# A two-layer hybrid block on one core: TensorE's build-time order made with a clock that counts each product's fixed part and each change of the array's form, and a new table of waits

## The chip, the cores and the metric

One core of one Trainium2 chip. The time is device microseconds of one execution of the whole program on that core. The kernel before has a median of 1361.12 us over three runs (1359.09 to 1361.54). Engines: TensorE (PE in the profile, its weight loads PEld), VectorE (DVE), ScalarE (ACT), GpSimd (POOL) and SyncE (SP), which issues most DMAs.

## The reference

Two layers of a block of a latent diffusion model. Its input are 256 latent rows and 256 context rows of 1024 numbers; the output are the latent rows after both layers.

```
for each layer:
  h  = adaLN(rms_norm(x));  hc = adaLN(rms_norm(ctx))      # scale, shift, gate from c and c_ctx
  A  = latent attention: q from a rank-256 part, k and v from a rank-128 part, 8 heads, rotary part
  B  = neighbourhood attention over a grid, window and context together, 8 heads, bias
  C  = Hyena: short convolution, two long convolutions (filters from a small MLP, by FFT)
  D  = gated linear attention, forward and backward, 4 heads, chunks of 64
  each branch * silu(its z) -> projection to 1024 -> * sigmoid(merge gate), summed
  x  = x + gate * rms_norm(sum @ w_out);   ctx likewise, in the first layer only
```

Context rows see only context rows in A and B; latent rows see both. All input and result types are fp32.

## The kernel before, in words

Nearly all of PE's time goes to products in fp32r. A factor `a` is split into a rounded part `ah` and a remainder `al` (for the incoming rows `hh` and `hl`, for weights `wh` and `wl`, for branch results `gh` and `gl`), and a product is three: `ah bh + ah bl + al bh`. The rounded part is a cast on ScalarE (L422, for weights L439 in `piece`), the remainder a subtraction on VectorE or GpSimd (`sub`, L380). Weights come as raw pieces of 512 KB through a pool of three buffers (`raw`, also `adaw` for adaLN); eight buffers hold split weights. PSUM has three pools: two buffers for the projections (`pj`, `pc`, `br`, `wo`), four for intermediate sums (`pa`, `sc`, `atp`, `go`, `ada`), two for transposes and small products (`ht`, `pt`, `ktp`, `kv`, `adat`).

PE's order is fixed while the program is built. Every part of the work is a generator that issues instructions and yields. A task that yields a number may go on when that many microseconds of PE's reckoned time have passed; `drive` (L312) takes the first task by priority that may go on, and where none may, it sets the reckoned clock to the earliest. The clock is moved by `mm` (L389: 512 columns of fp32r count 512/2400 = 0.2133 us; some callers pass a `cost`) and by `tr` (L403: 0.107 for a transpose). The numbers that tasks yield are in the table `WAIT` (L207), by name and layer; each stands for the time that other engines take before PE can use their result. The lowest priority has the long row of projections, branch products and merge gates of `layers`, which so fills the time of the others. Only PE's order is fixed like that (`manual_schedule`); the scheduler of the language sets the order of the other engines and queues for the PE order that it finds.

The tasks that matter here:

- `norm_in` (L633) turns the incoming rows, four groups of four transposes `ht` for each of the two streams. Behind each group VectorE and ScalarE apply scale and shift (`h`, L666 on ScalarE), ScalarE casts `hh`, and VectorE (second and fourth group) or GpSimd forms `hl`. Waits: `norm`, `norm_turn` ahead of the groups, `norm_step` between them.
- `latent_in` (L883) multiplies the turned rows by the weights of the low-rank parts (`pa`): it takes the four groups in turn. Behind it `latents` (L897) copies the parts `kr`, `xt` out of PSUM.
- `filters` makes the Hyena filters, products `f`, with waits `filt_...`.
- `ada_first` forms the first layer's scale and shift (`ada`, then two VectorE instructions `rows`, then `adat`), `ada_rest` (L600) the remaining parts, spaced by `ada_gap` and `ada_sum`.
- `unit` (L811) is one piece of attention: scores `sc`, maximum (L824), exponential (L826), scaling of `p` (L387), the wait `probs` or `probs2`, transposes `pt` and their copies. `q` in the first branch needs weights `wuq`, cast on ScalarE.
- `gla_dir` (L1238) is one direction of the linear attention for two heads: transposes `ktp`, a copy `kT` on ScalarE (L1270), the wait `gla_kT`, products `kv`, a chain of VectorE instructions `ut` over the chunks (L1289, L383), masked scores `atp`, four masking copies `at` on VectorE (L1314), the waits `gla_at` and `gla_scores`, and the products `go`, which need `at`.

Of the kernel before, what the change touches and what calls it, by code (L numbers as in the profile page):

```python
# [10 lines left out]
F32R = mybir.dt.float32r  # L11
# [114 lines left out]
def _layout(x, c, ctx, c_ctx, ada_w, ada_b, pre_g, post_g, w_in, mla_q_norm, mla_w_uq, mla_kv_norm, mla_w_ukv, na_rpb,  # L126
# [78 lines left out]


WAIT = {  # L207
    "ada_at0": (3.68, 7.47),
    "ada_at1": (6.0, 11.0),
    "ada_at2": (15.0, 17.0),  # L210
    "ada_at3": (17.5, 19.5),
    "ada_sum": (1.34, 0),
    "ada_load": (7.75, 9.57),
    "ada_gap": (4.19, 8.22),
    "norm": (3.44, 4.0),
    "norm_turn": (6.66, 5.25),
    "norm_ab": (0.16, 0.69),
    "norm_step": (0.65, 0.52),
    "filt_in": (3.1, 4.0),
    "filt_sin1": (6.0, 15.54),  # L220
    "filt_sin2": (6.0, 4.8),
    "filt_w3": (4.0, 4.49),
    "filt_step": (0.48, 0.82),
    "filt_sum": (10.0, 11.8),
    "filt_norm": (7.2, 15.6),
    "filt_dft": (0.3, 0.5),
    "filt_out": (1.82, 4.04),
    "probs": (5.63, 6.08),
    "probs2": (7.2, 7.7),
    "probs_out": (1.36, 0.94),  # L230
    "values_out": (1.14, 5.3),
    "latent_in": (2.81, 1.5),
    "latents": (10.0, 11.79),
    "latents_out": (5.62, 0.49),
    "mla_keys": (1.6, 1.78),
    "mla_v": (0.32, 0),
    "mla_k": (0.8, 2.25),
    "mla_q": (0.15, 0),
    "mla_q_out": (1.7, 1.04),
    "na_in": (2.87, 0.97),  # L240
    "hy_turn": (1.49, 4.79),
    "hy_turn_step": (0.35, 0.5),
    "hy_turn_out": (0.5, 0.67),
    "hy_dft": (1.57, 2.98),
    "hy_product": (12.59, 11.95),
    "hy_mid": (0.35, 0.81),
    "hy_out_step": (0.72, 0),
    "hy_order": (6.38, 0.9),
    "hy_out": (1.3, 1.0),
    "gla_in": (2.65, 0.67),  # L250
    "gla_logit": (1.02, 0.1),
    "gla_decay": (7.1, 2.9),
    "gla_dir": (6.31, 4.0),
    "gla_norm": (14.0, 4.73),
    "gla_turn": (0.03, 0.45),
    "gla_out": (1.66, 1.98),
    "gla_keys": (6.49, 5.03),
    "gla_kT": (0.9, 1.07),
    "gla_at": (0.5, 0.5),
    "gla_scores": (5.09, 7.57),  # L260
    "gla_o": (2.0, 1.05),
    "merged": (4.6, 3.55),
    "merged_step": (0.48, 0),
    "merged_out": (0.82, 1.24),
    "norm_first": (3.27, 8.0),
}


class Task:
    def __init__(self, gen, prio, ready):  # L270
        self.gen, self.prio, self.ready, self.cond, self.done = gen, prio, ready, None, False


class Block:
# [4 lines left out]
    def __init__(self, ctx, tc, dram, out):  # L279
        self.tc, self.nc, self.d, self.out = tc, tc.nc, dram, out  # L280
        pool = lambda name, bufs, **kw: ctx.enter_context(tc.tile_pool(name=name, bufs=bufs, **kw))
        self.const = pool("const", 1)
        self.small = pool("small", 1)
        self.hp = pool("hp", 1)
        self.mg = pool("mg", 4)
        self.raw = pool("raw", 3)
        self.wp = pool("wp", 8)
        self.gt = pool("gt", 8)
        self.gy = pool("gy", 4)
        self.s = pool("s", 20)  # L290
        self.tp = pool("tp", 15)
        self.tiny = pool("tiny", 6)
        self.dr = pool("dr", 1, space=bass.MemoryType.DRAM)
        self.pmm = pool("pmm", 2, space=bass.MemoryType.PSUM)
        self.pa = pool("pa", 4, space=bass.MemoryType.PSUM)
        self.pt = pool("pt", 2, space=bass.MemoryType.PSUM)
        self.n = 0
        self.clock = 0.0
        self.l = 0
        self.tasks = []  # L300
        self.ab = [self.small.tile([P, 2, 2, KT], F32, tag=f"ab{l}", name=f"ab{l}") for l in range(DEPTH)]
# [87 lines left out]
    def mm(self, out, lhsT, rhs, start=True, stop=True, skip=False, cost=None):  # L389
        self.nc.tensor.matmul(out, lhsT, rhs, start=start, stop=stop, skip_group_check=skip)  # L390
        if cost is None:
            cols = 1
            for w in rhs.shape[1:]:
                cols *= w
            cost = cols / 2400 if rhs.dtype == F32R else 4 * max(cols, 64) / 2400
        self.clock += cost

    def mm3(self, out, l, r, start, stop):
# [3 lines left out]

    def tr(self, out, in_):  # L403
        self.nc.tensor.transpose(out, in_, self.ident)  # L404
        self.clock += 0.107

    def rstd_of(self, halves):
# [1188 lines left out]
```

## Time and profile before

| | |
|---|---|
| median of 3 runs (lowest, highest) | 1361.12 us (1359.09, 1361.54) |
| the profiled execution, its span | 1358.52 us, 1356.7 us |
| granted TensorE clock, mean | 0.993 |
| PE busy | 1299.6 us, 96% |
| VectorE, ScalarE, GpSimd busy | 66%, 45%, 23% |
| DMA | 171.08 MB, 126 GB/s on the mean |

The times stand from the span's start. A row of a timeline gives the start, the duration, the engine, the line of the kernel, the operation, the result and its sources without their numbers, and in brackets how long the engine had stood idle before it and what ended that. Matmuls are pipelined: the distance of two starts is what one costs in a row of them. A line of a helper (L377, L380, L383, L387, L390, L404) serves many callers, so the names of the tiles tell the place.

### The profile page before, as it was taken

How to read it: one execution, taken by the hardware profiler on the slowest of the kernel's cores; microseconds unless marked ns; L12 is line 12 of the kernel's file. 1: busy time of each engine (PE TensorE's matmuls, PEld its weight loads, DVE VectorE, ACT ScalarE, POOL GpSimd, SP SyncE). 2: the span in 40 equal slices, each digit the busy share in tenths (PEclk: the TensorE clock that was granted, in tenths of full speed). 3: DMA queues.
4: the chain of work that ended last, by engine and by line, in shares of the span. 5: the costliest groups of instructions: out<-in, count | busy, mean ns of one | idle time of the engine just before them, and what ended most of it. 6: DMA issues, size and time to landing. Idle time of an engine off the chain costs nothing. (4 is left out here: it accounts for less than half of the span.)

```text
span 1356.7 us, 20161 instructions
## 1 busy us (share of the span) xinstructions
PE 1299.6 (96%) x7444; PEld 1023.7 (75%) x7444; DVE 889.4 (66%) x1660; ACT 607.1 (45%) x1282; POOL 318.3 (23%) x408
## 2 busy tenths in 40 slices
PE   5999999999999999999999999899999999999996
PEld 3877677777777776778767778787767899678875
DVE  5778666575143547676476597887579776768864
ACT  4655556233233332222344444575475456434552
POOL 2332213333030101124111123342123421121210
PEclk9999999999999999999999999999999999999999
DMA  9521222233243433324422352432135366434361
GB/s 350 214 93 40 93 70 77 94 110 109 94 155 124 145 120 108 124 94 139 142 77 80 114 192 85 138 106 99 48 115 158 115 211 212 156 101 153 118 208 63
DMA packets 55507, 171.08 MB, mean 126 GB/s; under 512 B 7470, under 2 KB 10128, under 8 KB 55408
## 3 DMA queue, kind: packets, MB, share of 16 engines
q1 hardware_dynamic: 49056, 153.31, 34.1%
q0 software_dynamic: 5440, 16.16, 3.8%
q8 instruction: 59, 0.97, 0.3%
q10 hardware_dynamic: 912, 0.31, 0.1%
q14 instruction: 40, 0.33, 0.1%
HBM read 163.45 MB, written 6.31 MB: 125 GB/s over the span
## 5 line engine op out<-in xcount | busy, mean ns | idle before, releaser
L380 DVE TENSOR_TENSOR wl<-raw,wh 128x512 fp32r<-128x512 f32 (+1 forms) x416 | 299.0, 740 | 191.2 <-ACT wh L439 186.3
L439 ACT CAST wh<-raw 128x512 fp32r<-128x512 f32 (+1 forms) x416 | 248.5, 617 | 285.1 <-DMA raw<-in_w_in 156.2
L390 PE MATMUL pc<-hh,wh 128*128 128x256 f32 (+1 forms) x688 | 239.8, 349 | 2.1 <-DVE kr L906 1.5
L390 PE MATMUL pc<-hh,wl 128*128 128x256 f32 (+1 forms) x688 | 229.8, 334 | 0.0
L390 PE MATMUL pc<-hl,wh 128*128 128x256 f32 (+1 forms) x688 | 229.3, 333 | 0.0
L390 PE MATMUL pj<-wh,hh 128*128 128x512 f32 x512 | 212.7, 415 | 1.5 <-ACT wh L439 0.8
L390 PE MATMUL pj<-wl,hh 128*128 128x512 f32 x512 | 200.6, 392 | 0.8 <-DVE wl L380 0.6
L390 PE MATMUL pj<-wh,hl 128*128 128x512 f32 x512 | 200.3, 391 | 0.0
L390 PEld LDWEIGHTS pc<-hh,wh 128*128 128x128 f32 x688 | 131.2, 191 | 25.6 <-issue 10.9
L390 PEld LDWEIGHTS pc<-hl,wh 128*128 128x128 f32 x688 | 131.2, 191 | 13.8 <-issue 2.4
L390 PEld LDWEIGHTS pc<-hh,wl 128*128 128x128 f32 x688 | 130.8, 190 | 13.3
L390 PEld LDWEIGHTS pj<-wh,hh 128*128 128x128 f32 x512 | 96.2, 188 | 32.3 <-issue 12.5
L390 PEld LDWEIGHTS pj<-wl,hh 128*128 128x128 f32 x512 | 96.4, 188 | 23.2 <-DVE wl L380 3.6
L390 PEld LDWEIGHTS pj<-wh,hl 128*128 128x128 f32 x512 | 96.1, 188 | 20.9
L380 POOL TENSOR_TENSOR gl<-y,gh 128x256 fp32r<-128x256 f32 (+1 forms) x44 | 36.6, 839 | 302.7 <-ACT gh L422 287.3
L826 ACT ACTIVATE p<-sc,mx 128x512 f32<-128x512 f32 (+1 forms) x96 | 59.0, 616 | 57.9 <-DVE mx L824 54.0
L390 PE MATMUL br<-wh,gh 128*128 128x512 f32 x192 | 77.2, 402 | 2.3 <-DVE gt L383 2.3
L390 PE MATMUL br<-wl,gh 128*128 128x512 f32 x192 | 75.1, 391 | 1.6 <-DVE wl L380 1.6
L390 PE MATMUL br<-wh,gl 128*128 128x512 f32 x192 | 74.9, 390 | 0.0
L1347 ACT ACTIVATE gt<-pj 128x512 f32<-128x512 f32 x48 | 28.6, 596 | 93.2 <-PE pj L390 93.0
L824 DVE TENSOR_REDUCE mx<-sc 128x1 f32<-128x512 f32 (+1 forms) x96 | 55.1, 591 | 11.5 <-PE sc L390 10.6
L377 POOL TENSOR_TENSOR merged<-merged,gt 128x512 f32<-128x512 f32 x24 | 33.1, 1385 | 83.8 <-DVE gt L383 83.8
(286 smaller groups left out, 2213.9 us busy)
## 6 DMA issues: line engine op xcount, KB each, us to landing
raw<-in_w_in SPq DMA_DIRECT2D x160, 512.0 KB, 3.6
adaw<-in_ada_w SPq DMA_DIRECT2D x36, 512.0 KB, 3.8
raw<-in_w_branch SPq DMA_DIRECT2D x32, 512.0 KB, 3.6
raw<-in_w_out SPq DMA_DIRECT2D x16, 512.0 KB, 4.4
adaw<-in_ada_w SPq DMA_DIRECT2D x24, 256.0 KB, 5.2
H<-filt POOLq DMA_DIRECT2D x16, 256.0 KB, 4.0
nab<-in_na_bias POOLq DMA_DIRECT2D x16, 256.0 KB, 3.0
raw<-in_w_in SPq DMA_DIRECT2D x8, 448.0 KB, 4.2
```

What stands on the lines that cost most here:

```text
L377: eng.tensor_tensor(out=out, in0=a, in1=b, op=ALU.add)
L380: eng.tensor_tensor(out=out, in0=a, in1=b, op=ALU.subtract)
L390: self.nc.tensor.matmul(out, lhsT, rhs, start=start, stop=stop, skip_group_check=skip)
L439: nc.scalar.copy(hi, raw[:, sl])
L824: nc.vector.tensor_reduce(out=mx, in_=ps[h][:, :nk], axis=AX.X, op=ALU.max, negate=True)
L826: nc.scalar.activation(p[h][:, :nk], ps[h][:, :nk], AF.Exp, bias=mx, scale=1.0, accum_out=sm)
L1347: self.nc.scalar.activation(gates[s, t], ps, AF.Tanh, scale=0.5)
```

## The change

No instruction is added or taken away, and all tiles, pools and engines are as before; a row's line numbers are 1 to 8 higher. What differs is the order in which `drive` issues PE's instructions, and with it the order that the scheduler gives the other engines.

The clock gets a fixed part of 32 columns for each fp32r product without a `cost` of its own, and 0.1 us wherever the form of the array differs from that of the product before: its rows (64 or 128) or its columns (32, 64 or 128).

```diff
         self.clock = 0.0
+        self.mode = (128, 128)
...
-            cost = cols / 2400 if rhs.dtype == F32R else 4 * max(cols, 64) / 2400
+            cost = (cols + 32) / 2400 if rhs.dtype == F32R else 4 * max(cols, 64) / 2400
+        mode = (64 if lhsT.shape[0] <= 64 else 128, 32 if out.shape[0] <= 32 else 64 if out.shape[0] <= 64 else 128)
+        if mode != self.mode:
+            self.mode = mode
+            cost += 0.1
         self.clock += cost
...
     def tr(self, out, in_):
         self.nc.tensor.transpose(out, in_, self.ident)
+        if self.mode != (128, 128):
+            self.mode = (128, 128)
+            self.clock += 0.1
         self.clock += 0.107
```

In the table most entries rise by about 6%. Those that move otherwise are, in the first layer, `ada_sum`, `ada_gap` (4.19 to 1.65), `norm`, `norm_turn`, `filt_sin2`, `mla_v`, `na_in`, `hy_mid`, `gla_turn` (0.03 to 1.89), `gla_kT`, `gla_at`, `gla_scores`, and in the second `ada_at1`, `norm`, `norm_step`, some of `filt_...`, `na_in`, `hy_mid`, `gla_keys`. Two of its lines:

```diff
-    "norm": (3.44, 4.0),
-    "gla_scores": (5.09, 7.57),
+    "norm": (4.8, 3.77),
+    "gla_scores": (4.1, 8.02),
```

Three places show what the new order does. The first is PE at the boundary of the layers, where the second layer begins: `ht` is the fourth group of transposes of the second stream, `pa` its products with the low-rank weights, `pc` a projection, `f` a product of the filters. Before:

```order
L390 MATMUL pa_8356<-wl_8089,hh_8202 128x192
L390 MATMUL pa_8356<-wh_8088,hl_8203 128x192
L404 MATMUL ht_8395<-ident,xn_8181 128x128
L404 MATMUL ht_8395<-ident,xn_8192 128x128
L404 MATMUL ht_8395<-ident,xn_8181 128x128
L404 MATMUL ht_8395<-ident,xn_8192 128x128
L390 MATMUL pa_8357<-wh_8088,hh_8202 128x192
L390 MATMUL pa_8357<-wl_8089,hh_8202 128x192
L390 MATMUL pa_8357<-wh_8088,hl_8203 128x192
L390 MATMUL pa_8357<-wh_8088,hh_8202 128x192
L390 MATMUL pa_8357<-wl_8089,hh_8202 128x192
L390 MATMUL pa_8357<-wh_8088,hl_8203 128x192
```

The same four transposes in the new order:

```order
L409 MATMUL ht_8366<-ident,xn_8169 128x128
L409 MATMUL ht_8366<-ident,xn_8180 128x128
L409 MATMUL ht_8366<-ident,xn_8169 128x128
L409 MATMUL ht_8366<-ident,xn_8180 128x128
L391 MATMUL f_2067_8378<-w3h_8134,a_1888_7688 128x512
L391 MATMUL f_2067_8378<-w3l_8135,a_1888_7688 128x512
L391 MATMUL pc_8359<-hh_7888,wh_8351 128x256
L391 MATMUL pc_8359<-hl_7889,wh_8351 128x256
L391 MATMUL pc_8359<-hh_7888,wl_8352 128x256
L391 MATMUL pc_8359<-hh_7888,wh_8351 128x256
L391 MATMUL pc_8359<-hl_7889,wh_8351 128x256
L391 MATMUL pc_8359<-hh_7888,wl_8352 128x256
```

Before, `pa` follows the fourth group at once, and six `pa` stand ahead of it; now two `f` and twelve `pc` (six of them shown) stand between the fourth group and the first `pa`.

The second place is ScalarE at the start of the program, around the casts `wh` of the first weights and the scaled rows `h`. Before:

```order
L666 ACTIVATE h_116_397<-ht_392,ab_99 128x256
L422 CAST hh_299<-h_114_387 128x2x256
L422 CAST hh_299<-h_116_397 128x2x256
L439 CAST wh_207<-raw_205 128x448
L439 CAST wh_211<-raw_205 128x448
L666 ACTIVATE h_124_450<-ht_402,ab_99 128x256
L439 CAST wh_217<-raw_215 128x448
L439 CAST wh_221<-raw_215 128x448
L422 CAST hh_299<-h_124_450 128x2x256
L666 ACTIVATE h_126_460<-ht_455,ab_99 128x256
```

The new order:

```order
L430 CAST hh_299<-h_111_377 128x2x256
L430 CAST hh_299<-h_112_382 128x2x256
L693 ACTIVATE arg_389<-argr_390 128x256
L737 CAST a_116_399<-arg_389 128x256
L674 ACTIVATE h_122_433<-ht_417,ab_99 128x256
L430 CAST hh_299<-h_122_433 128x2x256
L447 CAST wh_207<-raw_205 128x448
L447 CAST wh_211<-raw_205 128x448
L447 CAST wh_217<-raw_215 128x448
L447 CAST wh_221<-raw_215 128x448
L674 ACTIVATE h_124_443<-ht_438,ab_99 128x256
L430 CAST hh_299<-h_124_443 128x2x256
```

Before, two casts `wh` stand ahead of the third `h` and two behind it; now the third `h` is ahead of all four and the fourth, `h_124`, behind all four. The fourth group's transposes free the PSUM buffer that an `adat` on PE takes.

The third place is PE in the linear attention of the first layer, at the end of the masked scores `atp` of the second pair of heads. Before:

```order
L390 MATMUL atp_2845<-qp_2704,ktl_2700 64x64 x2
L390 MATMUL atp_2846<-qp_2704,ktl_2700 64x64 x2
L390 MATMUL atp_2845<-qp_2704,ktl_2700 64x64 x2
L390 MATMUL atp_2846<-qp_2704,ktl_2700 64x64 x2
L390 MATMUL go_2871<-gla_v_1874,at_2757 128x128
L390 MATMUL go_2872<-gla_v_1874,at_2758 128x128
L390 MATMUL go_2871<-gla_v_1949,at_2757 128x128
L390 MATMUL go_2872<-gla_v_1949,at_2758 128x128
L390 MATMUL go_2871<-gla_v_2130,at_2757 128x128
L390 MATMUL go_2872<-gla_v_2130,at_2758 128x128
```

The new order:

```order
L391 MATMUL atp_2883<-qp_2716,ktl_2712 64x64 x2
L391 MATMUL atp_2882<-qp_2716,ktl_2712 64x64 x2
L391 MATMUL atp_2883<-qp_2716,ktl_2712 64x64 x2
L391 MATMUL pj_2819<-wh_2604,hh_299 128x512
L391 MATMUL pj_2819<-wl_2605,hh_299 128x512
L391 MATMUL pj_2819<-wh_2604,hl_300 128x512
L391 MATMUL pj_2819<-wh_2610,hh_299 128x512
L391 MATMUL pj_2819<-wl_2611,hh_299 128x512
L391 MATMUL pj_2819<-wh_2610,hl_300 128x512
L391 MATMUL pj_2819<-wh_2614,hh_299 128x512
L391 MATMUL pj_2819<-wl_2615,hh_299 128x512
L391 MATMUL pj_2819<-wh_2614,hl_300 128x512
```

Before, the `go` of the first pair of heads stand right behind these `atp`, and the second pair's `go` much further on; now the first pair's `go` have gone ahead of these `atp`, and the second pair's `go` come after 15 `pj` and four `ada`, of which nine `pj` are shown.

## Rows read from the trace of the kernel before

**Rows 1.** The page: span, and busy time of each engine.

```profile
span 1356.7 us, 20161 instructions
...
PE 1299.6 (96%) x7444; PEld 1023.7 (75%) x7444; DVE 889.4 (66%) x1660; ACT 607.1 (45%) x1282; POOL 318.3 (23%) x408
```

**Rows 2.** What PE waited for: us in total, times, longest.

```profile
PE f L390 <- DMA pos<-in_w: 7.1, 1, 7.1
...
PE ktp L404 <- DVE ut L383: 2.8, 3, 1.5
...
PE pa L390 <- DVE o L374: 2.0, 1, 2.0
...
PE q L390 <- ACT wuq L422: 1.7, 2, 1.1
...
PE pt L404 <- DVE p L387: 1.3, 2, 0.7
...
PE hyt L404 <- ACT hy_u L1070: 0.5, 1, 0.5
```

**Rows 3.** Busy time by stretch; PEclk is the granted clock, then DMA share, GB/s.

```profile
893.00:896.50 3.50, 3.50 (x17) 3.31 (x17) 2.09 (x8) 2.08 (x7) 1.00 (x3) 0.52 0.15 57
```

**Rows 4.** PE's timeline, 880 to 897: start us, us; in brackets the idle before, releaser.

```profile
881.69 0.36 PE L390 MATMUL pc<-hh,wh 128*128 128x256 f32 x1 [1.51 <-DVE kr L906]
...
885.74 0.60 PE L404 MATMUL ht<-ident,xn 128*128 128x128 f32 x4
...
887.82 0.36 PE L390 MATMUL pa<-wh,hl 128*128 128x192 f32 x1 [0.61 <-DVE hl L380]
...
891.01 0.36 PE L390 MATMUL pa<-wh,hh 128*128 128x192 f32 x1 [1.16 <-ACT hh L422]
...
892.52 0.36 PE L390 MATMUL pa<-wh,hl 128*128 128x192 f32 x1 [1.04 <-DVE hl L380]
...
892.82 0.27 PE L390 MATMUL pa<-wl,hh 128*128 128x192 f32 x1
892.93 0.27 PE L390 MATMUL pa<-wh,hl 128*128 128x192 f32 x1
...
895.47 0.68 PE L390 MATMUL f<-w3h,a 128*128 128x512 f32 x1
...
896.59 0.28 PE L390 MATMUL pc<-hl,wh 128*128 128x256 f32 x1
896.71 0.28 PE L390 MATMUL pc<-hh,wl 128*128 128x256 f32 x1
```

**Rows 5.** VectorE's timeline: the subtraction hl at two places.

```profile
35.40 0.69 DVE L380 TENSOR_TENSOR hl<-h,hh 128x512 fp32r<-128x512 f32 x1
...
890.99 1.47 DVE L380 TENSOR_TENSOR hl<-h,hh 128x512 fp32r<-128x512 f32 x1 [0.20 <-ACT hh L422]
```

**Rows 6.** GpSimd's timeline at the boundary of the layers.

```profile
890.38 1.53 POOL L377 TENSOR_TENSOR fsm<-filt,filt 128x512 f32<-128x512 f32 x1 [1.48 <-DVE filt L764]
```

**Rows 7.** ScalarE's timeline at the start.

```profile
32.13 1.03 ACT L439 CAST wh<-raw 128x448 fp32r<-128x448 f32 x2 [4.95 <-DMA raw<-in_w_in]
33.07 0.56 ACT L666 ACTIVATE h<-ht,ab 128x256 f32<-128x256 f32 x1
```

**Rows 8.** PE's timeline at four earlier places.

```profile
33.68 0.61 PE L390 MATMUL adat<-par,rows 128*128 128x2 f32 x4 [1.25 <-ACT h L666]
...
137.61 0.41 PE L404 MATMUL pt<-ident,p 128*128 128x128 f32 x2 [0.69 <-DVE p L387]
...
150.41 0.39 PE L390 MATMUL pc<-hh,wh 128*128 128x512 f32 x1
150.64 0.39 PE L390 MATMUL pc<-hl,wh 128*128 128x512 f32 x1
...
262.91 0.73 PE L390 MATMUL atp<-qp,ktl 64*64 64x64 f32 x26
```

**Rows 9.** VectorE's timeline in the linear attention: the masking copies.

```profile
267.20 1.85 DVE L1314 COPY_PREDICATED at<-causal,atp 64x256 f32<-64x256 uint8 x4 [0.22 <-POOL at L1304]
```

More of the change, by code (lines that the diff above doesn't have):

```diff
@@ L207 @@
 WAIT = {
[L208 to L214, printed above, removed]
-    "norm": (3.44, 4.0),
[L216 to L258, printed above, removed]
@@ L259 @@
-    "gla_at": (0.5, 0.5),
-    "gla_scores": (5.09, 7.57),
[L261 to L265, printed above, removed]
+    "ada_at0": (3.9, 7.92),
+    "ada_at1": (6.36, 9.93),
+    "ada_at2": (15.9, 18.02),
+    "ada_at3": (18.55, 20.67),
+    "ada_sum": (0.71, 0.0),
+    "ada_load": (8.21, 10.14),
+    "ada_gap": (1.65, 8.71),
+    "norm": (4.8, 3.77),
+    "norm_turn": (5.59, 5.57),
+    "norm_ab": (0.17, 0.73),
@@ new lines @@
+    "norm_step": (0.69, 0.26),
+    "filt_in": (3.17, 3.48),
+    "filt_sin1": (6.36, 11.83),
+    "filt_sin2": (6.94, 5.09),
+    "filt_w3": (4.24, 3.41),
+    "filt_step": (0.51, 0.87),
+    "filt_sum": (10.6, 11.74),
+    "filt_norm": (7.63, 16.54),
+    "filt_dft": (0.32, 0.53),
+    "filt_out": (1.93, 4.28),
+    "probs": (5.97, 6.44),
+    "probs2": (7.63, 8.16),
+    "probs_out": (1.44, 1.0),
+    "values_out": (1.21, 5.62),
+    "latent_in": (2.98, 1.59),
+    "latents": (10.6, 12.72),
@@ new lines @@
+    "latents_out": (5.96, 0.52),
+    "mla_keys": (1.7, 1.89),
+    "mla_v": (0.67, 0.0),
+    "mla_k": (0.85, 2.39),
+    "mla_q": (0.16, 0.0),
+    "mla_q_out": (1.8, 1.1),
+    "na_in": (4.17, 1.7),
+    "hy_turn": (1.58, 5.08),
+    "hy_turn_step": (0.35, 0.53),
+    "hy_turn_out": (0.53, 0.71),
+    "hy_dft": (1.66, 3.16),
+    "hy_product": (13.35, 12.67),
+    "hy_mid": (0.37, 0),
+    "hy_out_step": (0.76, 0.0),
+    "hy_order": (6.76, 0.95),
+    "hy_out": (1.38, 1.06),
+    "gla_in": (2.81, 0.71),
@@ L266 @@
+    "gla_logit": (1.08, 0.11),
+    "gla_decay": (7.53, 3.07),
+    "gla_dir": (6.69, 4.24),
+    "gla_norm": (14.84, 5.01),
+    "gla_turn": (1.89, 0.48),
+    "gla_out": (1.76, 2.1),
+    "gla_keys": (6.88, 5.98),
+    "gla_kT": (0.63, 1.13),
+    "gla_at": (0, 0.53),
+    "gla_scores": (4.1, 8.02),
+    "gla_o": (2.12, 1.11),
+    "merged": (4.88, 3.76),
+    "merged_step": (0.51, 0.0),
+    "merged_out": (0.87, 1.31),
+    "norm_first": (3.47, 8.48),
 }
```

## The prediction

> **What bounds the kernel now.** I read the page's busy times first, then the list of what TensorE (PE) waited for, then PE's own timeline around the longest of these waits, and last the queues of the engines that PE waited for. PE is busy 1299.6 of 1356.7 us [rows 1], so 57.1 us are idle, and no other engine comes near. Of the 57.1, 7.1 lie before the first product, in the wait for a DMA [rows 2], and another part behind the last one; what an order can win or lose is what lies between. That is a long list of short waits, its kinds 1.3 to 2.8 us in sum where they are largest [rows 2], and with each goes a possible price of a second kind: after the waits at 887 to 892 us the granted clock is 0.52 in the next 3.5 us [rows 3], that is the lower of the two levels, 1.2 GHz, for nearly the whole stretch, and (1 - 0.52) x 3.5 = 1.7 us are lost. The reader is to see that PE's work is fixed and that only its waits and these stretches can move.
>
> **What the change is.** It removes and adds no instruction; the PE order has 6026 rows before and now. It makes PE's order anew. A 512-column product was counted as 0.2133 us and is now 0.2267; the two 512-column products at 150.41 and 150.64 stand 0.23 us apart [rows 8], so the new count is the truer one. Most entries of the table of waits rise by 6%, the same factor, and so mean about the same stretch of products as before. What is left are the entries that moved otherwise, and the sum goes by the places where the order then differs. The profiled execution took 1358.52 us (span 1356.7 and 1.8 around it), the median is 1361.12; I take the difference from the first and apply it to the second.
>
> **1. The boundary of the layers, -3.7 us.** Before, the fourth group of transposes of the incoming rows (`ht`, 885.74) is followed at once by the products `pa` that need its result, and PE waits before 887.82, 891.01 and 892.52 for 0.61, 1.16 and 1.04 us [rows 4]; the last of these three is 6.78 us behind the start of the transposes. The 1.7 us at the lower clock follow. In the new order the same four transposes come after 4 fewer `f` products (4 x 0.227), 6 fewer `pc` of 256 columns (6 x 0.12) and 6 fewer `pa` (6 x 0.11; both from the distance of two rows [rows 4]), some 2.3 us earlier, so at 883.4. With an unchanged 6.8 us their results serve at 890.2. Behind them now stand 2 `f` and 12 `pc` (0.45 + 1.44), then 30 `pa` that need only the first three groups (30 x 0.11 = 3.3) and two more that take the earlier half of the fourth's result: with the transposes' own 0.36, PE comes to the rest at 889.2, waits 1.0 to 890.2, and has 16 `pa` (1.8) to 892.0. Before it was through at 895.47, where the `f` row stands [rows 4], and by then it had done 6 `pc` less and 2 `f` more, worth 0.27. So 895.47 - 892.0 + 0.27 = 3.7 us, the lower clock's 1.7 in it. The wait of 1.51 before `pc` at 881.69 stays; it is for copies of `kr`, which the order leaves there. At least: only one of the three waits goes and the lower clock stays, -1. At most: all three, the restarts and the lower clock go, -6.
>
> A part of the 6.8 us is the subtraction `hl` on VectorE, 1.47 us at 890.99, while the same instruction took 0.69 at 35.40 [rows 5]; GpSimd worked on two SBUF operands beside the slow one [rows 6]. The Trainium skill (GPSIMD Engine Reference, Specifications) says that GpSimd's interfaces to SBUF are shared with VectorE and are contended for when a VectorE instruction has two SBUF inputs, as this one has; the trace agrees with its factor of 2. By that rule the subtraction would end 0.8 us sooner if GpSimd happens to be elsewhere in the new order, and the term would be -4.5; by the row, with the two beside each other as now, it is -3.7, which the sum takes.
>
> **2. The start, +1.0 us.** The first transposes come earlier, but on ScalarE four casts `wh` now stand ahead of the `h` for which the fourth group's PSUM buffer is waited for, where two stood before. The DMA lets the first begin at 32.13; two take 1.03 us, then `h` at 33.07 [rows 7], and PE's `adat` starts at 33.68 after 1.25 us idle [rows 8]. With four, `h` starts near 34.1 and `adat` 1.0 later, and all products up to 47 us hang on it in one row. If the earlier transposes give back what follows, it is -2; if the second raw piece is late, +2.
>
> **3. Attention of the first branch (100 to 215 us), -1.2 us.** `q` waited twice for the cast of its weights, 1.7 in all [rows 2]; two and three microseconds more of products stand ahead of it now, and the cast keeps its place in ScalarE's row, so -1.7. Against that, some seven of the transposes of the probabilities have one to three products less between scores and transposes. Two such transposes waited for the scaled probabilities already, 1.3 us in all [rows 2], 0.69 of it at 137.61 [rows 8], though others did not; each product taken away is 0.23 us of wait where the cover is gone. Two of seven units paying one product is +0.5; all seven paying two would be +3.2. Between -1.7 and +3 I stand near the waits that are seen: -1.2.
>
> **4. The scan's products `go` (245 to 312 us), +1.5 us.** `go` needs the masked scores `at`. The products `atp` end at 262.91 + 0.73 = 263.64 [rows 8], the last masking copy on VectorE at 267.20 + 1.85 = 269.05 [rows 9], 5.4 us later. Before, much more than this stood between them; now 15 products `pj` and four `ada` stand there: 15 x 0.227 + 4 x 0.12 = 3.9 us (an `ada` has 256 columns, as the `pc` at 896.59 and 896.71 [rows 4]). So PE waits 5.4 - 3.9 = 1.5. If VectorE, which has little else in this stretch, comes to the copies earlier, 0; if the other `go` (now ahead of the second `atp`) and the `kv`, with one group of three products less ahead of them, wait as well, +3. The wait for `ut` (2.8 in three [rows 2]) keeps its reason, a subtraction ahead of it on VectorE, and is left as it is.
>
> **5. Neighbourhood attention (664 to 820, and again in layer 2), +0.5 us.** Some twenty units lose two to four products of cover. Their cover was 8.4 to 9.1 us by the order and no wait on probabilities was seen there; it is now about 8. I take two units paying one product: +0.5; at most, with half of all paying two, +5.
>
> **6. The rest, -0.5 us.** One transposition in the convolution had waited 0.5 [rows 2] and has 1.1 us more ahead of it; the weight products of adaLN (`ada`) come closer together, with 2.3 instead of 5 us between a pair and the product that reads it. VectorE's two copies there take 0.4 us each and fit; taken at 0, at most +3 when VectorE's row delays them. Layer 2 from 900 us on has nearly its old order.
>
> Sum: -3.7 + 1.0 - 1.2 + 1.5 + 0.5 - 0.5 = -2.4; the profiled time would be 1356.1 and the median 1358.7 us. What this kernel's measurement can tell from no change is 0.2%, 2.7 us: below 1358.4 is faster, above 1363.8 slower.
>
> **Rivals.** *Deeper:* the boundary at its -6 and no new wait at `go`; -2.4 - 2.3 - 1.5 is -6.2 and gives 1354.9. For it: every wait at the boundary is one of the same kind, and VectorE is 66% busy on the mean. Against: the 5.4 us behind `atp` are measured [rows 8, 9]. *Given back:* at the boundary PE comes earlier to products whose inputs are as late as before (the copies `kr`, the weight casts for the next products), so that only the 1.7 us of the lower clock are won, or less; -1.7 + 1.0 - 1.2 + 1.5 + 0.5 - 0.5 is -0.4, 1360.7. For it: the wait for `kr` at 881.69 [rows 4] is untouched by the order. *Slower:* the covers of the probabilities' transposes. One chain decides it, scores, maximum, exponential, scaling, transposes; where its latency lies above about 6.3 us in the first branch and 8 in the neighbourhood branch, each missing product is 0.23 us of wait, and 27 units missing one and a half products are +9. Less the +1.0 counted for it, that is 1358.7 + 8 = 1366.7. For it: units with covers no smaller waited in the first branch. Against: in the neighbourhood branch none did.
>
> **How the numbers follow.** Forecast 0.43, its own range 1355.5 to 1361.5, a little under half of it below 1358.4; deeper 0.22; given back 0.15; slower 0.20. Faster is 0.20 + 0.22 = 0.42, within 0.2% is 0.23 + 0.15 = 0.38, slower 0.20. The 8-in-10 range reaches from a little under the deeper case to just short of the slower: 1352.5 to 1365.
>
> **What would show it.** In the new profile: no granted clock near 0.5 between 888 and 897 us, and the last 12 `pa` through some 3.5 us earlier, at 892 (right for 1); `adat` near 34.7 (2); `q` without a wait for its weights (3); PE waiting for the masking copy before `go` (4). Many small waits of `pt` for VectorE's `p` would make the forecast wrong, and so would a second stretch at the lower clock that is not there now.

## The result and the profile after

The changed kernel is slower: 1368.69 us (median of 7 runs, 1363.83 to 1372.1) against 1361.12 (7 runs, 1356.35 to 1362.92); the ratio is 1.0063, 95% interval 1.0046 to 1.0080. The forecast was 1358.7 and the range ended at 1365. Its profiled execution has a span of 1366.9 us, 10.2 more than before [rows 1]. The medians differ by 7.6 only: the execution that was profiled before took 1358.52 us, 2.6 less than its median, and this one 1368.78, about its median.

The page of the changed kernel, span and busy times:

```profile
span 1366.9 us, 20154 instructions
...
PE 1302.8 (95%) x7444; PEld 1025.1 (75%) x7444; DVE 889.5 (65%) x1660; ACT 604.9 (44%) x1282; POOL 323.7 (24%) x408
```

The 10.2 us divide at once: PE is busy 3.2 us longer with the same 7444 products, so more of them ran at the lower clock, and it is idle 64.1 us in place of 57.1. What it waited for in the changed kernel is shown by the rows that are new or larger (us in total, times, longest). The 1.3 us of `pt` for VectorE's `p` [rows 2] are gone:

```profile
PE adat L391 <- DVE rows L378: 4.2, 3, 2.0
PE pc L391 <- DVE zg L384: 3.9, 3, 2.3
PE ktp L409 <- DVE ut L384: 3.8, 3, 1.6
PE br L391 <- DVE gt L384: 3.3, 1, 3.3
...
PE adat L391 <- DVE rows L603: 2.5, 3, 1.4
PE pt L409 <- DVE pt L847: 2.5, 2, 1.7
PE q L391 <- ACT wuq L430: 2.2, 2, 1.2
...
PE ada L391 <- issue: 1.6, 1, 1.6
...
PE go L391 <- POOL st L388: 0.8, 1, 0.8
```

Where the time went is read from landmarks, places that PE passes in both orders: a wait for `glrT`, the first `pa` of the layers' boundary, the first `lat` behind it, and a pair `hd`. In the kernel before (PE's timeline; start first):

```profile
72.77 0.32 PE L404 MATMUL glrp<-ident,kr 128*96 128x128 f32 x1 [1.89 <-ACT glrT L940]
...
868.00 0.37 PE L390 MATMUL pa<-wh,hh 128*128 128x224 f32 x1 [1.98 <-DVE o L374]
...
900.78 0.60 PE L404 MATMUL lat<-ident,xt 128*128 128x128 f32 x4
...
941.05 1.10 PE L390 MATMUL hd<-filt,dft 128*128 128x512 f32 x2 [0.79 <-DVE k L380]
```

In the changed kernel:

```profile
77.45 0.32 PE L409 MATMUL glrp<-ident,kr 128*96 128x128 f32 x1 [1.89 <-ACT glrT L948]
...
878.65 0.37 PE L391 MATMUL pa<-wh,hh 128*128 128x224 f32 x1 [1.98 <-DVE o L375]
...
905.98 0.60 PE L409 MATMUL lat<-ident,xt 128*128 128x128 f32 x4
...
951.35 1.10 PE L391 MATMUL hd<-filt,dft 128*128 128x512 f32 x2 [0.80 <-DVE k L381]
```

So it is 4.7 us late at the first landmark, 10.7 at the second, only 5.2 at the third, and 10.3 at the last; from there on it stays so. PE's busy and idle time between these landmarks (us, before and changed):

| stretch | length | PE busy | PE idle |
|---|---|---|---|
| to the wait for `glrT` | 72.77, 77.45 | 56.43, 61.31 | 16.34, 16.14 |
| to the first `pa` | 795.23, 801.20 | 779.69, 781.15 | 15.54, 20.05 |
| to the first `lat` | 32.78, 27.33 | 28.46, 26.25 | 4.32, 1.08 |
| to the `hd` | 40.27, 45.37 | 38.83, 38.86 | 1.44, 6.51 |
| to the end | 415.65, 415.55 | 396.15, 395.21 | 19.50, 20.34 |

Three losses and one gain are to be explained: the start, which loses by slower products and not by more idle time; the stretch to 868 us; and the 5.1 us of waits behind the boundary, which take back most of the 5.4 won in it.

**The start.** In 20 to 40 us the changed kernel's granted clock is 0.74, before 0.93 (0.26 and 0.07 of 20 us, 5.2 and 1.4 lost). The first row is of the kernel before, the others of the changed kernel (PEclk, DMA share and GB/s last):

```profile
20.00:40.00 20.00, 16.57 (x141) 10.59 (x141) 14.16 (x37) 9.66 (x22) 4.81 (x7) 0.93 1.04 410
...
20.00:40.00 20.00, 16.82 (x106) 9.94 (x106) 14.36 (x31) 8.54 (x20) 5.00 (x6) 0.74 1.03 402
...
60.00:100.00 40.00, 38.12 (x169) 29.83 (x168) 33.22 (x63) 25.44 (x64) 16.82 (x19) 1.00 0.26 88
```

The last row gives a part back: before, the clock fell to 0.58 at 74 to 78 us, just behind the first landmark; now it doesn't. VectorE's timeline shows what stands in the way at the start:

```profile
27.55 1.38 DVE L384 SCALAR_TENSOR_TENSOR arg<-arg,argr 128x256 f32<-128x256 f32 x1
28.96 1.37 DVE L384 SCALAR_TENSOR_TENSOR argr<-arg 128x256 f32<-128x256 f32 x1
30.36 0.29 DVE L388 TENSOR_SCALAR argr<-argr 128x256 f32<-128x256 f32 x1
30.57 0.42 DVE L603 COPY rows<-ada 128x256 f32<-128x256 f32 x1
```

PE's timeline at the same place:

```profile
31.05 1.01 PE L391 MATMUL adat<-par,rows 128*128 128x2 f32 x4 [1.43 <-DVE rows L603]
31.92 0.72 PE L391 MATMUL pa<-wh,hh 128*128 128x448 f32 x1
```

The second filter product now comes behind the first transposes, so its sine chain (`arg`, `argr`) falls on VectorE ahead of the copy `rows` that `adat` waits for. Before, that product lay ahead of the wait for the adaLN weights (3.45 us at 19.94) and its chain was not in the way. The first `pa` behind it takes 0.72 us, where before it took 0.47: it runs at the lower clock, which is 0.50 from 28 to 36 us.

The two instructions of the chain take 1.38 and 1.37 us here, in all 1.9 more than before, which is more than the 1.43 that `adat` waits. VectorE's rows before:

```profile
22.04 0.42 DVE L383 SCALAR_TENSOR_TENSOR arg<-arg,argr 128x256 f32<-128x256 f32 x1
22.49 0.43 DVE L383 SCALAR_TENSOR_TENSOR argr<-arg 128x256 f32<-128x256 f32 x1
```

In the changed kernel GpSimd works beside them:

```profile
27.19 2.86 POOL L381 TENSOR_TENSOR hl<-h,hh 128x512 fp32r<-128x512 f32 x2 [3.16 <-DVE arg L388]
```

**The stretch to 868 us.** The `adat` of the later adaLN parts stand 2.3 us behind their `ada` now and wait three times, 4.2 us in all. VectorE's timeline at the longest:

```profile
449.39 1.30 DVE L381 TENSOR_TENSOR wl<-raw,wh 128x512 fp32r<-128x512 f32 x2 [2.74 <-ACT wh L447]
450.60 0.41 DVE L378 TENSOR_TENSOR rows<-rows,ada 128x256 f32<-128x256 f32 x1
```

VectorE was free 2.74 us before this, and PE's `ada`, which `rows` reads, ended near 446.3. But in VectorE's order the weight split `wl` stands ahead of `rows`, and `wl` waits for a cast on ScalarE, which began at 448.74 after waiting 3.66 us for the raw weights' DMA. PE's `adat` started at 451.07 after 1.95 us idle: `adat` so waits for a DMA of other weights.

That is not all of this stretch. `br` waits 3.29 us for `gt` at 798 us, before 1.94, and in the 20 us behind it the granted clock is 0.92, 1.6 us lost, where before nothing was lost. Against that the convolution's `hyt` no longer waits for `cv` (2.06 before).

**The boundary.** The waits for `hh` and `hl` are gone, as is the lower clock at 893 us; from `pa` to `lat` it is 27.3 us instead of 32.8. Then PE stands before `pc` for 2.34 us. VectorE's timeline there:

```profile
907.88 2.51 DVE L381 TENSOR_TENSOR wl<-raw,wh 128x512 fp32r<-128x512 f32 x2 [0.89 <-ACT wh L447]
910.31 1.75 DVE L381 TENSOR_TENSOR filt<-filt,filt 128x512 f32<-128x512 f32 x1
911.99 0.41 DVE L384 SCALAR_TENSOR_TENSOR zg<-zg,pc 128x256 f32<-128x256 f32 x1
```

GpSimd's timeline in the same stretch:

```profile
906.46 3.38 POOL L378 TENSOR_TENSOR fsm<-filt,filt 128x512 f32<-128x512 f32 x2 [0.20 <-DVE filt L375]
909.80 1.71 POOL L378 TENSOR_TENSOR fabs<-fabs,fabs 128x512 f32<-128x512 f32 x1
```

Two splits that take 1.30 us at 449 us (above) take 2.51 beside GpSimd's sums of the filter, and `zg`, which empties the PSUM buffer that the next `pc` needs, is behind them. Behind the splits stands a subtraction `filt` of 1.75 us; the next one of its kind, at 913.10 with GpSimd done, takes 0.68. Together that is 2.3 us more, as much as `pc` waits; that the wait would go without GpSimd's sums is an estimate from these rows, and no run took the sums away.

### The profile page after: what moved, and what is told of

Read it like the earlier page. It is cut to its first block, busy times and chain, and to the rows that moved or that the text cites. A ratio compares the mean times of both kernels' runs of the same rounds, so it can differ in the third digit from the quotient of the medians.

```text
span 1366.9 us, 20154 instructions
## 1 busy us (share of the span) xinstructions
PE 1302.8 (95%) x7444; PEld 1025.1 (75%) x7444; DVE 889.5 (65%) x1660; ACT 604.9 (44%) x1282; POOL 323.7 (24%) x408
## 5 line engine op out<-in xcount | busy, mean ns | idle before, releaser
L391 PEld LDWEIGHTS pc<-hh,wh 128*128 128x128 f32 x688 | 131.0, 190 | 28.3 <-issue 10.3
```

## The experiments

All were timed in five rounds beside the kernel before, 4 to 12 runs each, on four chips, on which the kernel before had medians of 1359.8 to 1362.1 us. So one kernel is compared with another by their ratios to the kernel before:

| kernel | us | ratio, 95% interval |
|---|---|---|
| changed kernel | 1368.69 | 1.0063 (1.0046, 1.0080) |
| start_back | 1366.65 | 1.0037 (1.0023, 1.0051) |
| gap_back | 1370.63 | 1.0078 (1.0060, 1.0096) |
| gla_back | 1372.35 | 1.0087 (1.0068, 1.0106) |
| norm_back | 1374.58 | 1.0100 (1.0087, 1.0113) |
| filt_back | 1373.93 | 1.0106 (1.0086, 1.0125) |
| clock_only | 1386.46 | 1.0189 (1.0166, 1.0211) |
| fixed_only | 1384.97 | 1.0183 (1.0162, 1.0204) |
| form_only | 1377.31 | 1.0121 (1.0100, 1.0142) |
| wait102 | 1369.55 | 1.0073 (1.0052, 1.0093) |
| table_only | 1381.81 | 1.0159 (1.0135, 1.0182) |
| before_norm | 1362.88 | 1.0023 (1.0008, 1.0037) |
| before_norm_filt | 1356.27 | 0.9971 (0.9953, 0.9990) |
| sum_late | 1374.18 | 1.0086 (1.0065, 1.0106) |
| start_sum | 1369.10 | 1.0061 (1.0037, 1.0085) |

### One place of the new order undone at a time

**start_back.** In the changed kernel:

```diff
-    "ada_sum": (0.71, 0.0),
+    "ada_sum": (1.42, 0.0),
...
-        yield self.wait("norm_turn")
+        yield 7.08 if l == 0 else self.wait("norm_turn")
```

> The changed kernel with the first 140 products of the program in the old order again (norm_turn of the first rows 7.08, ada_sum 1.42), all the rest in the new order. Theory: the changed kernel loses 3 us by 100 us, since the second filter product now stands behind the first transposes, VectorE's sine chain so falls ahead of the copy rows, and PE works at the lower clock from 26 to 36 us instead of 19 to 23. Then this kernel is about 3 us faster than the changed one (near 1365.5), with a granted clock of about 0.93 between 20 and 40 us. Rival: the start only shifts waits that return at the next joint (72 to 77 us); then it is within 1 us of the changed kernel, 1368.

The clock is 1.00 in 20 to 40 us and the first landmark as early as before; PE's timeline of this kernel:

```profile
72.68 0.31 PE L409 MATMUL glrp<-ident,kr 128*96 128x128 f32 x1 [1.88 <-ACT glrT L948]
...
873.79 0.55 PE L391 MATMUL pa<-wh,hh 128*128 128x224 f32 x1 [1.98 <-DVE o L375]
```

4.8 us are back at 73 us and 4.9 at 868, as the theory has it and more. In the whole time it is 0.26% faster than the changed kernel, 3.5 us by the ratios and 2.0 by the medians; the two intervals just overlap. In the profiled run 2.9 us came back later as stretches at the lower clock: the mean clock from this `pa` on for 18 us is 0.82, in the changed kernel's 0.91, and from 1300 to 1365 us 0.95 in place of 0.97.

**gap_back.** `"ada_gap": (1.65, 8.71)` to `(4.45, 8.71)`.

> The changed kernel with ada_gap of the first layer at 4.45 (the old value times 1.06) instead of 1.65. Theory: 4.2 us of PE's new waits are adat waiting for VectorE's rows, which stands in VectorE's row behind a weight split that waits for a DMA; with about 5 us of products between, they vanish, and the stretch at the lower clock at 477 us too: 4 to 6 us faster than the changed kernel, 1363 to 1365. Rival: the closer ada only move other waits of this stretch about; then 0 to 1.5 us.

The waits for `rows` of the later parts fall from 4.2 to 0.2 us, but the time is not lower. PE's timeline shows the new one:

```profile
293.60 1.01 PE L391 MATMUL adat<-rows,par 128*2 128x256 f32 x2 [3.80 <-DVE ut L384]
```

The rival holds in kind: another `adat` now stands behind VectorE's chain `ut`, and `hyt` waits 2.7 for `cv` again, as it did before the change (2.1).

**norm_back.** The second layer's incoming rows:

```diff
-        yield self.wait("norm_first" if l == 0 else "norm")
+        yield self.wait("norm_first") if l == 0 else (3.66, 4.25)[self.l]
...
-        yield self.wait("norm_turn")
+        yield self.wait("norm_turn") if l == 0 else (7.08, 5.58)[self.l]
...
-    "norm_step": (0.69, 0.26),
+    "norm_step": (0.69, 0.55),
```

> The changed kernel with the waits of the incoming rows of the second layer as they were (norm 3.66 and 4.25, norm_turn 7.08 and 5.58, norm_step 0.55). Theory: what the new order wins at 888 to 897 us (3.3 us of waits and 1.2 of clock) it gives back at 912 to 945 us, where PE waits for zg behind the late filters; with the old waits both go and the time is within 1 us of the changed kernel. Rival: the loss at 912 to 945 has another reason; then this kernel is 4 us slower than the changed one, 1372.5.

The landmarks of this kernel:

```profile
876.79 0.37 PE L391 MATMUL pa<-wh,hh 128*128 128x224 f32 x1 [1.98 <-DVE o L375]
...
909.41 0.60 PE L409 MATMUL lat<-ident,xt 128*128 128x128 f32 x4
...
952.26 1.10 PE L391 MATMUL hd<-filt,dft 128*128 128x512 f32 x2 [0.79 <-DVE k L381]
```

`pa` to `lat` is 32.6 us, as before the change (32.8), but `lat` to `hd` is 42.9 and not the 40.3 of before. The loss behind the boundary is half there without the gain: the theory that the one is the other's price falls, and the rival is nearer: 5.0 us slower than the changed kernel by the ratios (5.9 by the medians).

**gla_back.** `gla_turn`, `gla_kT`, `gla_at`, `gla_scores` of the first layer to 0.03, 0.96, 0.53, 5.41.

> The changed kernel with gla_turn, gla_kT, gla_at and gla_scores of the first layer as they were (0.03, 0.96, 0.53, 5.41). Theory: the new waits before go (0.8) and before the ada at 302 us, which needs a PSUM buffer that go frees (1.6), go: 2 to 2.5 us faster than the changed kernel, 1366.4. Rival: ktp waits for ut as before and takes their place: within 1 us.

Neither: 0.24% slower than the changed kernel, with intervals that overlap. The waits of `go` and of the `ada` at 302 us are gone, and PE waits elsewhere (the profiled run, 1378.8 us, is the slowest of the six):

```profile
292.58 1.17 PE L391 MATMUL kv<-gla_v,kT 64*64 64x128 f32 x24 [2.65 <-ACT kT L1278]
```

**filt_back.** The second layer's `filt_in`, `filt_sin1`, `filt_w3`, `filt_sum` to 4.25, 16.51, 4.77, 12.54.

> The changed kernel with the second layer's filter waits (filt_in, filt_sin1, filt_w3, filt_sum) as they were, times 1.0625. Theory: the 2.7 us lost between 905 and 960 us (waits for zg, scores, pt) come from the filter's VectorE and GpSimd work, which the new entries put beside the first gates; then these waits go and it is 2 to 3 us faster than the changed kernel, 1366. Rival: they come from the earlier products of the incoming rows and stay: within 1 us of the changed kernel.

Both fall: 5.9 us slower than the changed kernel by the ratios (5.2 by the medians), with a wait of 4.60 before the scores in PE's timeline:

```profile
909.19 0.39 PE L391 MATMUL pc<-hh,wh 128*128 128x256 f32 x1 [2.49 <-DVE zg L384]
...
932.21 4.71 PE L391 MATMUL sc<-k,q 128*128 128x512 f32 x9 [4.60 <-ACT q L430]
```

So, of the five groups of entries put back, two (`norm`, `filt`) cost 5 to 6 us, `gla` and `adat`'s distance nothing that can be told apart, and only the start may give 2 to 3.5 us back. That is at most half of the 0.63%; the rest had to be looked for in the clock itself and in the order as a whole.

### The clock and the table apart

**clock_only.** The new clock; every entry of the old table times 1.0625.

> The new clock with the old table, every entry times 1.0625: the fixed part and the changes of form are counted, nothing is fitted anew. Theory: the clock is not what costs; the loss is in the entries that were set anew (norm_turn, ada_sum, ada_gap, gla_..., filt_...). Then it is within 0.3% of the kernel before (1357 to 1364). Rival: the clock itself, which now counts 0.1 us at each change of form, takes cover away wherever forms change (attention, ada, linear attention); then it is as slow as the changed kernel, 1366 to 1370.

My theory falls by 26 us, and the rival's 1370 is passed by 16. The largest waits of PE in this kernel:

```profile
PE adat L391 <- DVE ut L384: 6.2, 2, 5.2
PE sc L391 <- ACT q L430: 4.7, 1, 4.7
PE pc L391 <- DVE zg L384: 3.8, 4, 2.7
PE hyt L409 <- DVE cv L384: 3.8, 1, 3.8
```

Three of them, those before `adat`, `sc` and `hyt`, are the waits that gap_back and filt_back brought in; `pc` waits as long in the changed kernel. The new entries take away about 17 of these 26 us (1.89% against 0.63%).

**fixed_only** (`cost += 0.1` and the 0.1 in `tr` set to 0, table as in clock_only) and **form_only** (old `cols / 2400`, old table, 0.1 us for each change of form).

> The new clock's fixed part of 32 columns without its 0.1 us for a change of form; old table times 1.0625. If the fixed part or any shift costs: near 1386, as with both. If the forms' 0.1 us made the loss: near 1360.

> The old clock and the old table unscaled, with only the 0.1 us for each change of form added. If the forms made the loss of the scaled table: near 1386. If any shift costs: also 1370 to 1388. If the forms are harmless: 1357 to 1364.

Each part costs alone: 1.8% and 1.2%. It isn't the one or the other. fixed_only also has the rescaled table, form_only the old one, so the two don't add up to clock_only.

**wait102.** The kernel before; every entry of its table times 1.02.

> The kernel before with its old clock and every entry of its table times 1.02, nothing else. Theory: the table is fitted to one order of this kernel, and any shift of the reckoned time, whatever its reason, moves about a thousand places of the order and costs; the new clock with the scaled table was such a shift (1386). Then this is 1370 to 1388 too. Rival: it was what the new clock counts that cost; then a shift by 2% is within 0.4% of the kernel before, 1355 to 1365.

0.73% slower, with the reckoned clock and its costs untouched; a little less than was said, but clear of the rival's 1365. Counted in the built programs by the name and shape of the result, some 1100 of the 6024 places of PE's order hold another product than before, with the new clock and the scaled table some 1200, and in the changed kernel some 1400: how many places moved doesn't tell what it costs. This is one shift, of one size and one way; whether one of -1% or -2% costs as much was not tried.

**table_only.** The old clock; the new table divided by 1.0625.

> The old clock with the new table divided by 1.0625. Theory of the fit: the new entries belong to the new clock's order and are worth nothing to the old one's: 1365 to 1385. Rival: the new entries are truer latencies and good with either clock: 1352 to 1362.

The new entries are no truer latencies: under the old clock they cost 1.6%.

### The boundary's gain by itself

**before_norm.** The kernel before with

```diff
-        yield self.wait("norm_first" if l == 0 else "norm")
+        yield self.wait("norm_first") if l == 0 else (4.52, 3.55)[self.l]
...
-        yield self.wait("norm_turn")
+        yield self.wait("norm_turn") if l == 0 else (5.26, 5.24)[self.l]
...
-    "norm_step": (0.65, 0.52),
+    "norm_step": (0.65, 0.245),
```

> The kernel before, old clock, with only the waits of the second layer's incoming rows set anew (norm 4.52 and 3.55, norm_turn 5.26 and 5.24, norm_step 0.245, which are the new ones divided by 1.0625). Theory: the boundary's gain is real and by itself: 3 us between 868 and 905 us, of which 0 to 1 is given back by 960; 2 to 3 us faster than the kernel before, 1357.5. Rival: PE comes earlier to gates that are as late as before and loses the gain again between 905 and 960 us; then no change, 1360.

**before_norm_filt.** The same, and the second layer's `filt_in`, `filt_sin1`, `filt_w3`, `filt_sum` at 3.28, 11.13, 3.21, 11.05.

> As the last one, and the second layer's filter waits set anew too (divided by 1.0625). If the filter entries make the loss between 905 and 960 us, this is 2 to 3 us slower than the one with the rows' waits alone; if not, the two agree within 1 us.

The first is 0.2% slower than the kernel before: it wins 3.4 us from `pa` to `lat` and loses it to waits for `zg` (2.34) and `q` (2.38). With the filter entries, of which I had expected nothing or harm, it is 0.29% faster than the kernel before and so faster than both. Its landmarks:

```profile
867.63 0.38 PE L390 MATMUL pa<-wh,hh 128*128 128x224 f32 x1 [1.98 <-DVE o L374]
...
894.02 0.60 PE L404 MATMUL lat<-ident,xt 128*128 128x128 f32 x4
...
936.67 1.10 PE L390 MATMUL hd<-filt,dft 128*128 128x512 f32 x2 [0.79 <-DVE k L380]
```

26.4 and 42.7 us: the gain at the boundary is 6.4, of which the stretch behind it takes 2.4, where the changed kernel lost 5.1. A part of both gains is the clock in these single profiled runs: in the 18 us from `pa` on it is 1.00 here, 0.83 in before_norm and 0.91 in the kernel before and in the changed kernel, so 1.6 of the 6.4 us are clock, and all of the 3.0 by which the two runs differ there. The profiled run is also the fastest of ten, 3.6 us under the median.

### The distance of `adat` alone

**sum_late.** In the changed kernel's `ada_rest`:

```diff
-                    yield self.wait("ada_gap")
+                    yield max(4.45, self.wait("ada_gap")) if half else self.wait("ada_gap")
```

**start_sum**: the same with start_back's edit.

> The changed kernel in which only the product adat, which reads VectorE's rows, comes at least 4.45 us of reckoned time behind the second pair of ada products; the spacing of the ada among themselves stays new. Theory: adat so near behind ada is what waits (4.2 us, and 1.6 us of lower clock at 477 us), so 4 to 5 us less between 312 and 530 us and 1364 in all. Rival: the order of this stretch is so changed by it that other waits come in, as with the old ada_gap (312 to 530 us then 221 us, as against 225); then 1367 to 1371.

> The last one with the old start as well. If the two places are independent: the 3 us that the old start gave up to 100 us, and the 4 to 5 of the late adat, near 1361; if not, 1365 or more.

In sum_late the waits for the later `rows` fall to 0.7 us, but the time is not lower: 0.23% above the changed kernel's, with intervals that overlap. It is the rival's way, past its 1371. start_sum is at the changed kernel's ratio, so the start's gain does not add to one from the late `adat`. That `adat` waited for `rows` is seen in the trace; that the changed kernel would be faster without these waits is not shown by any run, since each way to remove them moved many other places as well.

## Why the prediction was wrong, step by step

**What the change is.** "Most entries of the table of waits rise by 6%, the same factor, and so mean about the same stretch of products as before": this is the step that failed. The factor 544/512 is that of 512 columns. A product of 256 columns counts 288/256, 12.5% more, a transpose no more than before, and products with a cost of their own and changes of form scale otherwise again. clock_only is the test of this step, the new clock with every entry raised by the same factor: it should have been near the kernel before and is 1.9% slower. The old table held for the old order only; 2% on every entry already costs 0.7%, about what the changed kernel lost. The sum went by the differences that were large enough to be looked at, a few per engine, and took all others for equal, while some 1400 places had moved.

By stretch, said and measured in the profiled runs: the start +1.0 and +4.7; from there to the boundary (3 to 6 of the prediction) +0.3 and +6.0; the boundary -3.7 and -5.4; behind it, where the order was called nearly the old one, 0 and +5.1. The runs show these sizes and the waits in them; which of the moved places makes the 6.0, no run took apart.

**1, the boundary.** Right in kind and larger than said: 5.4 us from `pa` to `lat` where -3.7 stood, the three waits and the lower clock [rows 3, 4] gone. The subtraction `hl` of the fourth group was no faster, 1.38 us at 898.02 beside GpSimd again, but PE no longer waited for it. The rival "given back" was right in effect, 5.1 us by `hd`. Its reason is half right: PE waits for gates behind VectorE's filter work, but norm_back shows 2.6 us of the loss without the gain, and before_norm_filt a gain of 6.4 with 2.4 given back. The waits behind the boundary in the changed kernel are 2.9 for `zg`, 0.99 for `q` and 1.67 for a copy of `pt`; which product's place makes the last two stays open.

**2, the start.** +1.0 was said, +4.7 measured at the first landmark. The four casts `wh` ahead of `h` were the wrong term: they run from 34.26 to 36.22, and PE does not wait for the `h` behind them. Instead `adat` waits for `rows` behind the filter's sine chain, which GpSimd's work beside it makes three times as long, and the lower clock costs 3.8 us more than before between 20 and 40 us; PE's idle time up to the landmark is not longer. The prediction names the earlier transposes but not the filter product that they passed, and counts no lower clock here. It also called the waits 2.8 us in sum where they are largest; the one for the adaLN weights in this stretch is 3.4.

**3, attention of the first branch.** The waits for `wuq` did not go, 2.2 us after 1.7 [rows 2]: in ScalarE's timeline the cast stands right behind an exponential `p` (155.49, then the cast at 156.16), as it did before. The `pt` that were to wait more wait less; the 1.3 us for `p` are gone. PE is idle 3.5 us from 100 to 215 us, before 4.4, which is near the -1.2 that was said, for other reasons: luck.

**4, `go`.** PE waits 0.8 us, not 1.5, and for GpSimd's `st`, not for the masking copies, 0.2. `ada` at 302 us waits 1.57, for which the trace names no releaser; that it waits for a PSUM buffer of `go` is argued only. Undoing the entries took both away and did not make the kernel faster.

**5 and 6.** No `pt` of the neighbourhood branch waits more, so the rival "slower" had the wrong place. `adat` behind `ada` was priced at 0, at most 3, with "VectorE's two copies there take 0.4 us each and fit": the copies do, but VectorE's row ahead of them waits for a DMA, and 4.2 us came. `br` waits 3.3 for `gt` instead of 2.3, with a lower clock behind it, and the convolution's `hyt` lost its wait of 2.1 for `cv`; neither was named by a step.

## What to carry to other kernels

A table of waits that was set by trials fits one order and one clock. A truer clock with the same table rescaled is a new, untried order, and here it lost 1.9%; judge it after the table is set anew, and beside a control that shifts everything by a per cent or two. Where an order moves in a thousand places, the few that one can read do not give the sum, and the range must take in what an arbitrary shift of that kernel costs (the one tried here: 0.7%). Before a consumer is moved nearer to its producer, read what stands ahead of the producer on its engine: here a copy of 0.4 us came late because a split of other weights before it waited for their DMA.

## What the runs showed of the hardware

The same wait of PE is not always followed by the same clock: behind the wait of 1.98 us before `pa`, the next 18 us have a granted clock of 0.91 in the changed kernel, 0.82 in start_back and 1.00 in sum_late, with PE busy 16.92 to 16.93 us in all three. At 0.82 that is 0.18 of 18 us, 3.2 us, lost. Whether this spreads the runs of one kernel can be read in part from the mean granted clock of each run. In before_norm_filt it goes with the time: six runs at 0.993 or 0.994 took 1352.7 to 1356.6 us, four at 0.988 to 0.990 took 1356.8 to 1361.9. In the changed kernel it doesn't: the fastest run, 1363.83 us, has 0.988 and the slowest, 1372.1, has 0.991, so what spreads these seven runs over 8 us stays open.

VectorE's instructions that read two SBUF operands lengthen beside GpSimd's: the sine chain's `arg` and `argr` from 0.42 and 0.43 to 1.38 and 1.37 us, two weight splits from 1.30 to 2.51, `filt` from 0.68 to 1.75. GpSimd's own lengthen less: two `hl` take 2.53 us at the start of the kernel before and 2.86 here.
